# Turning six of eight token tiles to channel-major by VectorE block transposes and transfers inside SBUF

## The chip, the cores and the metric

The kernel runs on one core of a Trainium2 chip. The metric is the device time of one execution in microseconds; the time before is the median of three runs. Work is done by TensorE (PE: matrix products and transposes, with its weight load PEld), VectorE (DVE), ScalarE (ACT), GpSimd (POOL), and by transfers that are issued mostly from SyncE's queue (SP). Everything runs in float32, where a product of two matrices is made of three products of their high and low parts.

## The reference, cut to what matters

One decoder layer on 16 meta tokens and 1024 sequence tokens with 1024 channels. The change lies between the output projection with its LayerNorm and the up-projection of the feed-forward net:

```python
mixed = sigmoid(g_attn) * y_attn + sigmoid(g_conv) * y_conv
h = layer_norm(ALPHA * h + mixed @ w_out, ln1_g, ln1_b)
up = causal_dwconv(h @ ffn_w_up, ffn_dw, ffn_dw_b)        # 3 taps over tokens
u, g = split(up, 2)
f = (gelu(g) * u) @ ffn_w_down
return layer_norm(ALPHA * h + f, ln2_g, ln2_b)
```

The LayerNorm runs over channels, so it wants tokens on the partitions and channels along the row. The product `h @ ffn_w_up` contracts over channels, so it wants channels on the partitions. Between the two, `h` must be turned.

## The kernel before, in words

The stage `w_out` takes the 1024 sequence tokens as eight tiles of 128, in the written order 3, 7, 2, (-1), 6, 0, 4, 1, 5; "-1" is the pair of rows that the convolution needs from before the sequence. For each tile `out_rows` loads its residual row tile from DRAM into one of two places in `RT` (the first half of `OB`), makes the product in two halves of 512 channels on TensorE (`product`, line 1339, 24 products of 512 columns a half), adds the residual and takes statistics on VectorE (lines 1342 and 1343), normalises the tile (line 1364), and stores it to DRAM (`h1d`) for the later residual.

`turn` then turns a normalised tile: eight 128x128 transposes on TensorE (line 1378) into two banks of PSUM, and eight ScalarE activations (line 1388) that apply the gain and bias of the LayerNorm, which are now one number per partition, and write into `FA` (`h1F(sub, h, k)`). A tile's turn is emitted inside the next tile's `out_rows`, behind the product of one of its halves: `behind=[last]` puts the transposes after that product in TensorE's order, and the next half's first product after them. The list `ahead` says which tile is due. Tile 5, the last, is turned in the first pass of the up-projection.

`FA` holds `h` for two halves of the tokens, `sub` 1 (tiles 2, 3, 6, 7) and `sub` 0 (the two edge rows, tiles 0, 4, 1, 5); tiles 0 to 3 have h = 0 and tiles 4 to 7 have h = 1. The up-projection is a two-by-two block scheme with seven products in place of eight: B11, B21, B22 are blocks of `h` (a half of the channels for one h), and BT1 to BT4 are sums of blocks. `form_t2`, `form_t3` and `form_t4` make the sums on VectorE (line 1288), and `split_of` splits each operand into a high part (ScalarE, line 1279) and a low part (VectorE, line 1284). `form_t2` subtracts first B11 from B12 and then B11 from B22, so it needs all channels of the tiles with h = 1. EARLY is the first half of `sub` 0, tiles 0 and 4; LATE is tiles 1 and 5.

Three things set the order of work around the change:

- `rank(...)` gives instructions a priority (smaller goes first) by which the builder orders each engine's queue against its own estimate of the times. The queue it writes is then executed in order.
- `line(ins)` chains instructions: each is put after the one lined before it in VectorE's order. The sums and statistics of tiles 0, 4, 1 and 5 are lined (`pin`, line 1334), and so are the low parts, the sums of blocks, and the first splits of the up-projection's weights. The dictionary `work` says which of them is emitted between the two halves of which tile:

```python
    work = {0: [(w_first, 2), (split_of, 1, B11), (split_of, 1, B21), (split_of, 1, B22)],
            4: [(w_first, 3), (split_of, 1, BT2), (w_first, 3), (form_t4, 1)],
            1: [(form_t3, 1), (split_of, 0, B11, EARLY), (form_t2, 0, EARLY), (w_first, 5)],
            5: [(w_first, 6)]}
```

- Places in SBUF: the second half of `OB` holds `T2_AT` and, for tile -1, its two rows (columns 3072 to 4095); `OC` and `RHC` hold later the operands of `sub` 1 (`B_AT`).

The products of a half wait for one of three PSUM banks with the tag "mm". Every load and store of this stage is issued from SP (line 113).

Of the kernel before, what the change touches and what calls it, by code (L numbers as in the profile page):

```python
# [25 lines left out]
AF = mybir.ActivationFunctionType  # L26
# [3 lines left out]
P = 128  # L30
D = 1024
KC = D // P
# [29 lines left out]
SUB = [(0, 258), (258, HW)]  # L62


RK_TURN, RK_SPLIT, RK_EVAC, RK_START, RK_QKV, RK_RESID, RK_ATT = 450, 500, 600, 1000, 10000, 20000, 30000
# [36 lines left out]
def tile_hybrid_layer(  # L102
# [3 lines left out]
    nc = tc.nc  # L106
# [5 lines left out]
    def load(o, i):  # L112
        return nc.sync.dma_start(out=o, in_=i)
# [5 lines left out]
    def f32(ap):  # L119
        return ap.bitcast(F)  # L120

    def after(ins, first):

        tc.add_manual_dep(ins.ins, first.ins.name, mybir.DependencyInfo(
            mybir.DependencyClass.NoSync, mybir.DependencyReason.SCHED_ONLY), reason="order of work")

    @contextmanager
    def rank(p):

        saved = tc.cur_priority  # L130
        tc.cur_priority = p
        yield
        tc.cur_priority = saved
# [10 lines left out]
    RHC = arena.tile([P, 8384], R, name="RHC")  # L144
    RHO = arena.tile([P, 8384], R, name="RHO")
    OB = arena.tile([P, 4 * U], F, name="OB")
# [49 lines left out]
    cols = const.tile([P, N_COLS], F, name="cols")  # L196
# [19 lines left out]
    g1col = lambda k: colA[:, 58 + k:59 + k]  # L216
    b1col = lambda k: colA[:, 66 + k:67 + k]
# [60 lines left out]
    def split(raw, hi, lo, quick=False, behind=None):  # L278
        ins = nc.scalar.copy(hi, raw)  # L279
        if behind is not None:  # L280
            after(ins, behind)
        return (nc.vector if quick else nc.gpsimd).tensor_tensor(lo, raw, f32(hi), OP.subtract)  # L282
# [391 lines left out]
    bias = ap.tile([P, 2, NH // 2, KW], F, name="bias")  # L674
# [58 lines left out]
    for r in range(2):  # L733
        rows = slice(r * HD, (r + 1) * HD)
# [13 lines left out]
    src = ps[:16, :P].rearrange("p (g d) -> p g d", d=HD)  # L748
    nc.scalar.copy(VA[:16, 0, :, 0], src)
    nc.vector.tensor_tensor(VA[:16, 0, :, 1], src, f32(VA[:16, 0, :, 0]), OP.subtract)  # L750
    for q4 in range(2):
# [4 lines left out]
        src = ps[:, :].rearrange("p (n g d) -> p n g d", g=2, d=HD)  # L756
# [16 lines left out]
    def load_q(g, i):  # L773
        m = 0 if i else 16
        t = ap.tile([P, 8 * P + 16], R, name="qt", tag="qt", bufs=3)[:, 16 - m:]
        for h in range(2):
            load(f32(t[h * HD:(h + 1) * HD]), dram(qd, g * HD * 8 * U + q_at(i) - m, [[8 * U, HD], [1, 8 * P + m]]))
        if m:
            pairs0.append(t[:, :16].rearrange("p (l r q) -> p l r q", l=2, r=4))
        return t[:, m:].rearrange("p (u l h x) -> p l u h x", l=2, u=2, h=2)  # L780
# [7 lines left out]
    ahead = chunks_done[first_chunk + 2 * KC + 7]  # L788
# [6 lines left out]
    for h in range(NH):  # L795
        g, r = divmod(h, 4)
        o = ps[:2, h * 16:(h + 1) * 16]
# [34 lines left out]
    for g in range(NKV):  # L832
# [3 lines left out]
        src = ps[:16].rearrange("p (r q) -> p r q", r=4)[:, :, 0:2]  # L836
# [3 lines left out]
    for g in range(NKV):  # L840
        o = po[:, g * 8:g * 8 + 8]
# [21 lines left out]
    for i in range(NB):  # L863
        for g in range(NKV):
            q = load_q(g, i) if i else q0[g]
# [6 lines left out]
            for u in range(2):  # L872
# [3 lines left out]
                for h in range(2):  # L876
                    o = ps[:, h * KW:h * KW + w]
# [8 lines left out]
                if not i:  # L886
                    f = first[u]
                    src = ps[:, :2 * KW].rearrange("p (h c) -> p h c", h=2)
# [9 lines left out]
            for h in range(2):  # L898
                for u in range(2):
                    j = h * 2 + u  # L900
# [68 lines left out]
    OC = late.tile([P, 8320], R, name="OC")  # L969
# [169 lines left out]
    def two_rows(k, behind=None):  # L1139

        for t, a in enumerate(two_sum):
            m = pair[:, k, t:t + 1]
            if k == 0:
                nc.scalar.activation(a, wo_raw[k], AF.Copy, scale=m)
                continue
            ins = nc.vector.scalar_tensor_tensor(a, wo_raw[k], m, a, OP.mult, OP.add)
            if behind is not None:
                after(ins, behind)
# [74 lines left out]
    def h1_at(sub, i):  # L1223
        return 2048 * sub + i * (SUB[sub][1] - SUB[sub][0])

    def h1F(sub, h, k):
        o = h1_at(sub, h * KC + k)
        return FA[:, o:h1_at(sub, h * KC + k + 1)]
# [28 lines left out]
    def line(ins):  # L1257

        if lined:
            after(ins, lined[-1])  # L1260
        lined.append(ins)
        return ins
# [9 lines left out]
    def bsplit(sub, q, src, cs=slice(None)):  # L1272
        with rank(RK_SUMS):
            a = columns(sub, q)[0] - SUB[sub][0]
            x, y, _ = cs.indices(SUB[sub][1] - SUB[sub][0])
            x = max(x, a)
            hi, lo = (wide(bsum(sub, q, hl))[:, :, x - a:y - a] for hl in range(2))
            src = wide(src)[:, :, x:y]
            ins = nc.scalar.copy(hi, src)
            if (sub, q) in ((0, BT2), (0, BT4), (0, BT1), (0, BT3)):  # L1280
                if high:
                    after(ins, high[-1])
                high.append(ins)
            line(nc.vector.tensor_tensor(lo, src, f32(hi), OP.subtract))
# [5 lines left out]
    def blocks(sub):  # L1290

        return [quadrant(sub, kk, h) for kk in range(2) for h in range(2)]
# [3 lines left out]
    def form_t2(sub, cs=slice(None)):  # L1296
        b11, b12, b21, b22 = blocks(sub)
        bsub(b11, b12, b11, cs)
        bsub(T2_AT[:, :b22.shape[1]], b22, b11, cs)

    def form_t3(sub, cs=slice(None)):
        b11, b12, b21, b22 = blocks(sub)
        bsub(b12, b22, b12, cs)

    def form_t4(sub, cs=slice(None)):
        b11, b12, b21, b22 = blocks(sub)
        bsub(b21, T2_AT[:, :b22.shape[1]], b21, cs)

    def split_of(sub, q, cs=slice(None)):
        b11, b12, b21, b22 = blocks(sub)  # L1310
        src = {B11: b11, B21: b21, BT2: T2_AT[:, :b22.shape[1]], BT4: b21, BT1: b11, BT3: b12, B22: b22}[q]
        bsplit(sub, q, src, cs)
# [76 lines left out]
        return behind[-1] if behind else None  # L1389


    RING = [RHO[:, i * 1024:(i + 1) * 1024] for i in range(4)]
    RING += [None] * 4
    RING += [RHO[:, 6208 + i * 1024:6208 + (i + 1) * 1024] for i in range(2)]
    ring_next, W2 = [0], []

    def wsplit(src):
# [4 lines left out]
        else:  # L1402
            i = (i - 2) % len(RING)
            if RING[i] is None:
                RING[i] = wsp_p.tile([P, D], R, name="ws", tag=("whi", "wlo")[i % 2])
            t = RING[i]
        hi, lo = t[:, 0:512], t[:, 512:1024]
# [59 lines left out]
    def edges():  # L1467
        with rank(RK_TURN):
            first, second = (FA[:, h * 2064:h * 2064 + 2064].rearrange("p (k n) -> p k n", n=258)[:, :, 0:2]
                             for h in range(2))  # L1470
            for t, c, op in ((edge, 58, OP.mult), (first, 66, OP.add)):
                line(nc.vector.tensor_tensor(first, t, colA[:, c:c + KC].unsqueeze(2).to_broadcast([P, KC, 2]), op))
            nc.vector.memset(second, 0.0)

    ahead = []
# [4 lines left out]
    for i in (3, 7, 2, -1, 6, 0, 4, 1, 5):  # L1480
        if i == -1:
            out_rows(i)
            continue
        rows = out_rows(i, ahead, work.get(i, ()))
        ahead = [None, (i, *rows)] if i == 3 else [(i, *rows)]
        if i == 3:
            two_rows(7, rows[2])
        if i == 7:
            for a, (hi, lo) in zip(two_sum, two_parts):
                after(split(a, hi, lo, True), rows[2])  # L1490
            two_stack.close()
            W2.append(wo_stack.enter_context(tc.tile_pool(name="w2", bufs=1, side="right", reuse_waits="tile")).tile(
                [P, 2048], R, name="W2"))
        if i == 0:
            form_t2(1)
        if i == 4:
            split_of(1, BT4)
            split_of(1, BT1)
            edges()
        if i == 1:  # L1500
            split_of(1, BT3)
            split_of(0, B21, EARLY)
            form_t3(0, EARLY)
            form_t4(0, EARLY)
# [64 lines left out]
    for c in range(FC):  # L1569
# [8 lines left out]
        for subs in passes:  # L1578
            last = subs == passes[-1]
            w_next = iter(range(7))  # L1580
            a, b = SUB[subs[0]][0], SUB[subs[-1]][1]
            i = max(a, 2)

            def at(t, a=a):
                return t[:, 254 + a:254 + b]
# [19 lines left out]
            def tt(*x):  # L1605
                with rank(RK_CHAIN):
                    return nc.vector.tensor_tensor(*x)
# [12 lines left out]
            ins = tt(c11[:, a:b], at(Z), u13[:, a:b], OP.add)  # L1620
# [23 lines left out]
            ins = tt(c22[:, i:b], c22[:, i:b], u13[:, i:b], OP.add)  # L1644
# [127 lines left out]
    rows, stats = {}, {}  # L1772
# [158 lines left out]
```

## Time and profile before

| | |
|---|---|
| median of 3 runs | 1236.12 us (1236.04 to 1236.16) |
| span of the profiled execution, first to last instruction | 1234.6 us |
| the profiled execution's own time beside it | not listed apart; the span is 1.5 us below the median |
| busy PE / DVE / ACT | 99% / 88% / 47% of the span |
| stage `w_out` (products from about 500 us, first up-projection product) | to 589.4 us |
| products of the up-projection | 589.4 to about 1017 us |
| products of the down-projection | 1017 us to the end |

A line of the trace's timeline gives the start and length in us, the engine, the line of the kernel, the operation, output <- inputs, shapes, how many such instructions follow each other (x8), and in brackets the idle time before it and what released it. A group line gives durations in ns as minimum/median/maximum. Records of TensorE overlap, since its products are pipelined: how far apart they start says more than how long each one lasts.

### The profile page before, as it was taken

The page shows a single profiled execution, that of the slowest core. Times are in us where ns is not written, and L with a number is a line of the kernel's source. Part 1 is how long each engine was busy: PE and PEld are TensorE (multiplying, and loading weights), DVE is VectorE, ACT ScalarE, POOL GpSimd, SP SyncE. Part 2 cuts the span into 40 slices and gives each one's busy share as a digit, 9 for nine tenths or more (in the row PEclk, how much of TensorE's full clock was granted, in tenths as well). Part 3 has the DMA queues.
Part 4 walks back from the last instruction along what each step waited for, and adds up shares of the span by engine and source line. Part 5 has one row for each costly group of instructions (what it writes and reads, how often), then busy time and mean ns, then how long its engine had stood idle before and what let it go on. Part 6 is the DMA issues. An engine that isn't in the chain of part 4 may idle for free.

```text
span 1234.6 us, 21810 instructions
## 1 busy us (share of the span) xinstructions
PE 1225.2 (99%) x8568; PEld 1141.5 (92%) x8568; DVE 1085.2 (88%) x1842; ACT 584.7 (47%) x1065; POOL 15.6 (1%) x20
## 2 busy tenths in 40 slices
PE   9999999999999999999999999999999999999997
PEld 8999989999999999888999999999999998888886
DVE  8899989999879798659899999998999986996697
ACT  7532336654255223345755545555455554445331
POOL 1000000000000010000000000000000000000000
PEclk9999999999999999999999999999999999999999
DMA  7396834412255655322255555554455568988722
GB/s 282 74 298 151 210 98 116 127 55 73 82 158 163 183 140 144 104 85 87 66 171 207 191 187 205 188 183 142 172 203 190 178 239 304 391 315 312 256 86 85
DMA packets 109152, 213.02 MB, mean 173 GB/s; under 512 B 31883, under 2 KB 46779, under 8 KB 108922
## 3 DMA queue, kind: packets, MB, share of 16 engines
q1 hardware_dynamic: 93050, 200.56, 49.5%
q10 hardware_dynamic: 16000, 11.07, 2.9%
q8 instruction: 67, 1.10, 0.4%
q14 instruction: 35, 0.29, 0.1%
HBM read 149.98 MB, written 62.70 MB: 172 GB/s over the span
## 4 chain that ended last, share of the span: by engine, by line
PE 98%; DVE 1%; ACT 0%; issue 0%; DMA 0%; POOL 0%; DVEq 0%; POOLq 0%
PE px L1599 14%; PE py L1599 9%; PE ps_x L1745 9%; PE ps_z L315 8%; PE ps_z L314 8%; PE ps_z L310 8%; PE ps_z L1745 8%; PE pw L1599 5%; PE pz L1599 5%; PE ps_p L310 2%; PE ps_p L314 2%; PE ps_p L315 2%; PE ps_w L310 2%; PE ps_w L315 2%; PE ps_w L314 2%; PE ps_z L550 2%
## 5 line engine op out<-in xcount | busy, mean ns | idle before, releaser
L707 DVE SCALAR_TENSOR_TENSOR FA<-cin,cols,FA 128x1026 f32<-128x1026 f32 x120 | 152.2, 1277 | 0.9
L315 PE MATMUL ps_z<-RHO,wlo 128*128 128x256 f32 (+2 forms) x324 | 103.5, 320 | 0.0
L314 PE MATMUL ps_z<-RHO,whi 128*128 128x256 f32 (+2 forms) x324 | 103.4, 319 | 0.0
L315 PE MATMUL ps_z<-RHC,wlo 128*128 128x256 f32 (+2 forms) x324 | 103.4, 319 | 0.0
L314 PE MATMUL ps_z<-RHC,whi 128*128 128x256 f32 (+2 forms) x324 | 103.4, 319 | 0.0
L310 PE MATMUL ps_z<-RHO,whi 128*128 128x256 f32 (+2 forms) x324 | 103.3, 319 | 0.0
L310 PE MATMUL ps_z<-RHC,whi 128*128 128x256 f32 (+2 forms) x324 | 103.2, 319 | 0.0
L279 ACT CAST whi<-wr 128x1024 fp32r<-128x1024 f32 x37 | 38.9, 1050 | 107.4 <-PE ps_z L314 85.5
L1408 ACT CAST RHO<-wr 128x512 fp32r<-128x512 f32 x92 | 55.3, 619 | 25.3 <-DVE wr L1426 11.7
L1409 DVE TENSOR_TENSOR RHO<-wr,RHO 128x512 fp32r<-128x512 f32 x92 | 61.8, 684 | 5.1 <-ACT RHO L1408 5.0
L310 PEld LDWEIGHTS ps_z<-RHO,whi 128*128 128x128 f32 x324 | 60.9, 188 | 4.3
L314 PEld LDWEIGHTS ps_z<-RHO,whi 128*128 128x128 f32 x324 | 61.0, 188 | 4.2
L310 PEld LDWEIGHTS ps_z<-RHC,whi 128*128 128x128 f32 x324 | 60.9, 188 | 4.1
L314 PEld LDWEIGHTS ps_z<-RHC,whi 128*128 128x128 f32 x324 | 61.0, 188 | 4.0
L315 PEld LDWEIGHTS ps_z<-RHO,wlo 128*128 128x128 f32 x324 | 60.9, 188 | 4.0
L315 PEld LDWEIGHTS ps_z<-RHC,wlo 128*128 128x128 f32 x324 | 61.0, 188 | 3.9
L1426 DVE TENSOR_TENSOR wr<-wr 128x512 f32<-128x512 f32 x88 | 59.9, 681 | 0.2
L282 DVE TENSOR_TENSOR wlo<-wr,whi 128x1024 fp32r<-128x1024 f32 x35 | 42.7, 1220 | 11.8 <-ACT whi L279 11.4
L1611 ACT COPY FA<-px 128x514 f32<-128x514 f32 (+2 forms) x23 | 13.2, 572 | 70.7 <-PE px L1599 70.6
L1408 ACT CAST ws<-wr 128x512 fp32r<-128x512 f32 x60 | 36.1, 618 | 18.8 <-DVE wr L1426 10.7
L714 ACT ACTIVATE FA<-ps_z,cols 128x258 f32<-128x258 f32 (+2 forms) x48 | 26.1, 544 | 39.4 <-PE ps_z L315 36.6
L1599 PE MATMUL px<-OA,RHO 128*128 128x258 f32 (+1 forms) x336 | 43.8, 279 | 0.0
(491 smaller groups left out, 3488.2 us busy)
## 6 DMA issues: line engine op xcount, KB each, us to landing
wr<-in_w_up_dram SPq DMA_DIRECT2D x44, 512.0 KB, 4.6
wr<-in_w_z_dram SPq DMA_DIRECT2D x30, 512.0 KB, 3.9
fd<-FA SPq DMA_DIRECT2D x44, 256.0 KB, 2.4
OB<-in_w_down_dram SPq DMA_DIRECT2D x19, 512.0 KB
qt<-qd SPq DMA_DIRECT2D x28, 256.0 KB, 4.1
td<-OB SPq DMA_DIRECT2D x12, 512.0 KB
sums<-fd SPq DMA_DIRECT2D x12, 512.0 KB, 7.6
sd<-sums SPq DMA_DIRECT2D x12, 512.0 KB
```

Of the source, the lines that this page charges most:

```text
L279: ins = nc.scalar.copy(hi, raw)
L282: return (nc.vector if quick else nc.gpsimd).tensor_tensor(lo, raw, f32(hi), OP.subtract)
L310: ins = nc.tensor.matmul(ps, ah, bh, start=i == 0, stop=False)
L314: nc.tensor.matmul(ps, ah, bl, start=False, stop=False)
L315: last = nc.tensor.matmul(ps, al, bh, start=False, stop=i == n - 1)
L707: nc.vector.scalar_tensor_tensor(acc[c], cin[:, j:j + U], wc, acc[c], OP.mult, OP.add)
L714: nc.scalar.activation(t, ps, AF.Tanh, bias=bcol(14 + i), scale=0.5)
L1408: nc.scalar.copy(hi, src)
L1409: ins = nc.vector.tensor_tensor(lo, src, f32(hi), OP.subtract)
L1426: ins = nc.vector.tensor_tensor(*x)
L1599: ins = nc.tensor.matmul(o, x[:, ks], bmat(sub, q, hl, k), start=first and k + j == 0, stop=k == 3 and j == 2, skip_group_check=not first)
L1745: nc.tensor.matmul(bank[:, cs], l[:, ts], r[:, ws], start=first and a and x + k == 0, stop=z and x == len(ops) - 1 and k == 2, skip_group_ ...
```

## The change

Six tiles (3, 7, 2, 6, 0 and 4) are no longer turned by TensorE. The new `turn_dma` does it in three steps:

1. One VectorE transpose of the tile's 1024 columns in blocks of 32x32, written into a block of 1024 columns in the second half of `OB` (columns 2048 on for tiles 3, 7, 2 and 6, columns 3072 on for tiles 0 and 4). Each 32x32 block is turned in place; the blocks of one row of partitions hold 32 tokens.
2. Sixteen transfers within SBUF, issued from SP, each of 32 partitions with 1 KB: they bring the 4x4 arrangement of blocks into its turned order, in a place of the tile's own in `OC` or `RHC` that is free then.
3. The same eight ScalarE activations as before, now with SBUF as the source and with four runs of 32 columns each.

The tiles 1 and 5 are turned as before. The list `ahead` stays empty where the last tile was turned in the new way. For tiles 0 and 4 the VectorE transpose is lined; tile 0's stands right behind its normalisation, tile 4's behind the low parts of BT4 and BT1 of `sub` 1.

```diff
+    TURN_AT = {3: (OC, 4144, 2048), 7: (OC, 5168, 2048), 2: (OC, 6192, 2048), 6: (OC, 7216, 2048), 0: (RHC, 2096, 3072), 4: (RHC, 3120, 3072)}
+
+    def turn_dma(i, r):
+        t, o, b = TURN_AT[i]
+        blocks, cols = OB[:, b:b + 1024], f32(t[:, o:o + 1024])
+        with rank(RK_TURN):
+            ins = nc.vector.transpose(blocks.rearrange("p (q k j) -> p q k j", q=4, k=KC),
+                                      r.rearrange("p (k q j) -> p q k j", k=KC, q=4))
+            if i in (0, 4):
+                line(ins)
+            for a in range(4):
+                for q in range(4):
+                    load(cols[32 * q:32 * q + 32, a * 256:(a + 1) * 256],
+                         blocks[32 * a:32 * a + 32, q * 256:(q + 1) * 256])
+            h, jj = divmod(i, 4)
+            sub = 0 if jj < 2 else 1
+            a = 2 + jj * P - SUB[sub][0]
+            src = cols.rearrange("p (a k j) -> p k a j", a=4, k=KC)
+            for k in range(KC):
+                nc.scalar.activation(h1F(sub, h, k)[:, a:a + P].rearrange("p (a j) -> p a j", a=4), src[:, k],
+                                     AF.Identity, bias=b1col(k), scale=g1col(k))
...
         rows = out_rows(i, ahead, work.get(i, ()))
-        ahead = [None, (i, *rows)] if i == 3 else [(i, *rows)]
+        ahead = [] if i in TURN_AT else [(i, *rows)]
+        if i in TURN_AT and i != 4:
+            turn_dma(i, rows[0])
         if i == 3:
             two_rows(7, rows[2])
...
         if i == 4:
             split_of(1, BT4)
             split_of(1, BT1)
+            turn_dma(i, rows[0])
             edges()
```

## The prediction

> **What bounds the kernel now.** I read the page's head and its chain of waits first, then a table of busy time by stage around the change, then the timelines of TensorE, VectorE, ScalarE and the DMA queue there.
>
> ```profile
> span 1234.6 us, 21810 instructions
> PE 1225.2 (99%) x8568; PEld 1141.5 (92%) x8568; DVE 1085.2 (88%) x1842; ACT 584.7 (47%) x1065; POOL 15.6 (1%) x20
> PE 98%; DVE 1%; ACT 0%; issue 0%; DMA 0%; POOL 0%; DVEq 0%; POOLq 0%
> ...
> 542.00:554.00 12.00, 12.00 (x58) 10.03 (x57) 8.87 (x14) 4.77 (x11) 0.00 (x0) 1.00 0.39 103
> 554.00:566.00 12.00, 12.00 (x58) 10.02 (x57) 10.81 (x17) 6.74 (x14) 0.00 (x0) 1.00 0.25 89
> 566.00:578.00 12.00, 12.00 (x58) 10.03 (x57) 11.24 (x21) 6.35 (x13) 0.00 (x0) 1.00 0.23 88
> 578.00:592.00 14.00, 14.00 (x78) 12.10 (x78) 10.59 (x20) 6.36 (x17) 0.00 (x0) 1.00 0.23 77
> ```
>
> TensorE sets the time, 98% of the chain. But the four stage rows (columns: stretch, length, busy PE, PEld, DVE, ACT, POOL, clock, DMA share, GB/s) say something that the average of 88% hides: from 554 to 578 us VectorE is busy 22.05 of 24 us. The stage of the change has two nearly full engines; time taken off one can be used only as far as the other keeps up. The clock is 1.00 throughout and plays no part.
>
> **What TensorE gives back.** Columns: start, length, engine, line, operands.
>
> ```profile
> 521.98 0.40 PE L315 MATMUL ps_w<-whi,RHC 128*128 128x512 f32 x1
> 522.22 1.04 PE L1378 MATMUL ps_h<-cols,OB 128*128 128x128 f32 x8
> 523.01 0.48 PE L310 MATMUL ps_w<-RX,RHC 128*128 128x512 f32 x1
> 523.33 0.40 PE L314 MATMUL ps_w<-RX,RHC 128*128 128x512 f32 x1
> ...
> 583.03 1.03 PE L1378 MATMUL ps_h<-cols,OB 128*128 128x128 f32 x8
> ```
>
> Products start every 0.227 us elsewhere in this listing. Around one tile's eight transposes, the third product after 521.98 starts at 523.33, 1.35 us later, where two steps are 0.45: a turn costs TensorE 0.9 us, not the 8 x 0.27 that its records last. Three turns (3, 7, 2) stand ahead of tile 6's normalisation; those of 6, 0 and 4 stand behind the first halves of tiles 0, 4 and 1. Removing the six gives 6 x 0.9 = 5.4 us, 2.7 us of it before tile 0's first half is ready, all of it before tile 1's turn at 583.03. So 5.4 us (0.44%) is the ceiling.
>
> **What VectorE leaves of it.** From tile 0 on, VectorE's work is pinned one behind the other (`line`): every entry below waits for the one above.
>
> ```profile
> 545.03 0.81 DVE L1364 TENSOR_SCALAR OB<-OB,mv,sd 128x1024 f32<-128x1024 f32 x1
> 547.88 0.69 DVE L1342 TENSOR_TENSOR OB<-ps_w,OB 128x512 f32<-128x512 f32 x1 [2.03 <-PE ps_w L315]
> ...
> 549.21 1.27 DVE L1409 TENSOR_TENSOR W<-wr,W 128x512 fp32r<-128x512 f32 x2
> 550.41 2.35 DVE L1284 TENSOR_TENSOR OC<-FA,OC 128x1024 fp32r<-128x1024 f32 x2
> 552.68 1.22 DVE L1284 TENSOR_TENSOR RHC<-FA,RHC 128x1024 fp32r<-128x1024 f32 x1
> 554.22 0.69 DVE L1342 TENSOR_TENSOR OB<-ps_w,OB 128x512 f32<-128x512 f32 x1 [0.32 <-PE ps_w L315]
> ...
> 564.12 1.22 DVE L1284 TENSOR_TENSOR OC<-OB,OC 128x1024 fp32r<-128x1024 f32 x1
> ...
> 571.74 1.22 DVE L1284 TENSOR_TENSOR OC<-FA,OC 128x1024 fp32r<-128x1024 f32 x1
> 572.88 0.17 DVE L1472 TENSOR_TENSOR FA<-edge,cols 128x16 f32<-128x16 f32 x1
> ...
> 574.50 1.21 DVE L1288 TENSOR_TENSOR FA<-FA 128x1024 f32<-128x1024 f32 x1
> 575.82 0.70 DVE L1284 TENSOR_TENSOR RHC<-FA,RHC 128x520 fp32r<-128x520 f32 x1
> 576.56 0.70 DVE L1288 TENSOR_TENSOR FA<-FA 128x520 f32<-128x520 f32 x1
> 577.29 0.70 DVE L1288 TENSOR_TENSOR OB<-FA 128x520 f32<-128x520 f32 x1
> ...
> 581.11 0.81 DVE L1364 TENSOR_SCALAR OB<-OB,mv,sd 128x1024 f32<-128x1024 f32 x1
> ```
>
> The last row is tile 1's normalisation, ending at 581.92; TensorE transposes tile 1 at 583.03, so today VectorE is 1.1 us early. From 547.88 to 581.92 is 34.04 us of pinned work, with one wait for TensorE in it (0.32). The change lets it begin 2.7 us earlier (545.2), drops the 0.32, and adds the block transposes of tiles 0 and 4.
>
> A block transpose of 128x1024 fp32 isn't in the trace. Nearest rows: 1.22 us (L1284, same elements, two tensors) and 0.81 us (L1364, one tensor). Bounds: 0.81, and 2.44 if it took two passes. I take 1.22, one element a step like most of VectorE's rows.
>
> With no other wait, tile 1 is normalised at 545.2 + 34.04 - 0.32 + 2.44 = 581.4, and TensorE turns it there instead of at 583.03: gain 1.6 us, not 5.4. TensorE waits for VectorE first.
>
> **What the new way takes.** Of each turn's steps, after the block transpose: 16 transfers (32 partitions x 1 KB) issued one by one from SP, the last one's landing, then eight ScalarE evacuations, each reading all 16 pieces.
>
> ```profile
> L113 SPq DMA_DIRECT2D ed<-OB x1: 244/244/244, 536.2 to 536.2; - x1
> L113 SPq DMA_DIRECT2D v1d<-vrow x1: 297/297/297, 62.6 to 62.6; - x1
> L113 SPq DMA_DIRECT2D OB<-h0d x8: 319/320/341, 499.2 to 573.4; - x8
> L113 SPq DMA_DIRECT2D FA<-kd x4: 453/548/587, 53.3 to 61.3; - x4
> ...
> qd<-qsh SPq DMA_DIRECT2D x4, 1.0 KB, 1.8
> out_dram<-r SPq DMA_DIRECT2D x16, 256.0 KB, 2.0
> OB<-h0d SPq DMA_DIRECT2D x8, 512.0 KB, 3.2
> ...
> 496.59 0.42 ACT L1191 ACTIVATE RHC<-OB 128x256 fp32r<-128x256 f32 x1 [1.62 <-DVE OB L1186]
> 548.31 2.90 ACT L1388 ACTIVATE FA<-ps_h,cols 128x128 f32<-128x128 f32 x8 [3.90 <-PE ps_h L1378]
> 551.25 1.05 ACT L1279 CAST RHC<-FA 128x1024 fp32r<-128x1024 f32 x1
> ```
>
> The issue time (ns, min/median/max) hardly follows the size: 244 for 2 rows, 297 for 8, 320 for 128, 453 at least for 64. I take 0.33 a transfer with the gap, as 32 rows lie between the 8 and the 128; ends 0.244 and 0.453. Landing (last column, us): 1.8 for 1 KB to 3.2 for 512 KB; I take 2.0. So the lag from the end of a block transpose to the last landing is D = 16 x 0.33 + 2.0 = 7.3 us (5.7 to 10.4). The evacuations stay at 2.90 us for eight (SBUF source, by the 0.42 row at most 3.4). On the old path the first followed the transposes at once.
>
> Two pinned VectorE entries need a turn that comes late:
>
> - **Wait A, tile 6.** 552.68 (L1284 into RHC) is the low part of B22 of the second half, which needs all of tiles 6 and 7 and ScalarE's cast (1.05). VectorE gets there 4.80 us after its start: 545.2 + 4.8 = 550.0. Tile 6's normalisation ends at 545.84 - 2.7 = 543.1, its transpose at 544.35, so B22 is ready at 544.35 + D + 2.90 + 1.05 + 0.1 = 548.4 + D. Wait: D - 1.6 = 5.7 us.
> - **Wait B, tile 4.** Its transpose is pinned behind the entry at 571.74; 3.7 us of old work (572.88 to 576.56) and 0.7 (first subtraction) cover it before the second `form_t2` subtraction (577.29), which needs all of tile 4: wait D + 2.9 - 4.4 = D - 1.5 = 5.8 us.
>
> Behind both stand tile 1's second-half sum, its normalisation and so the transposes at 583.03, for which TensorE waits in order, as tile 5's second half is tied behind them. Sum: 5.7 + 5.8 - 1.6 = +9.9 us (2D - 4.7). Ends by D: +6.7 to +16.1; a transpose of 0.81 or 2.44 shifts by -1.2 or +3.7 (three of them lie in these sums), slower evacuations by +1.0.
>
> Other pieces, with their cover. The tiles' shared OB block makes tile 7's transpose wait for tile 3's landing (512.8, the end of its normalisation, + 1.2 + 7.3 = 521.3); behind it on VectorE stand the two edge-row splits, needed by TensorE's products with `sel`:
>
> ```profile
> 511.98 0.80 DVE L1364 TENSOR_SCALAR OB<-OB,mv,sd 128x1024 f32<-128x1024 f32 x1
> ...
> 519.92 2.36 DVE L282 TENSOR_TENSOR OC<-two,OC 128x1024 fp32r<-128x1024 f32 x2
> ...
> 528.56 2.02 PE L1353 MATMUL ps_w<-OC,sel 128*2 128x512 f32 x8
> ...
> 534.10 0.81 DVE L1364 TENSOR_SCALAR OB<-OB,mv,sd 128x1024 f32<-128x1024 f32 x1
> ```
>
> They end at 521.3 + 1.2 + 2.4 = 524.9, the products now come at 526.8: nothing, 1.9 us spare. SP issues 96 more transfers (32 us in some 66), ahead of the loads of residual rows: tile 2's normalisation (534.9 - 1.8) plus 1.2 and 16 x 0.33 ends the issue at 539.6, tile 0's rows then land at about 543.1 (0.3 + 3.2), needed at 545.2; without those 2 us a late load adds its excess. The added 3.1 MB lie in stages with a DMA share of 0.23 to 0.39. POOL has no work here. After tile 5 all moves with TensorE; I find nothing that gives the loss back.
>
> Median: 1236.12 against a span of 1234.6; I add the 9.9 to the median: **1246.0 us**.
>
> **A rule against the row.** The trace's issues take 0.244 to 0.32 us each, 16 of them 3.9 to 5.1, more than a landing of 2.0. The Trainium skill, "DMA: Bandwidth & Descriptors", section "Issuing engines are not separate DMA queues", has it that the time a sequencer spends on starting a DMA is usually small relative to the DMA itself. By that rule the change would come out at no change, the first rival below; by the trace's rows 16 small transfers in a row are bound by it.
>
> **Rivals.**
> 1. *Issue costs nothing in a row* (no change). If issues ran on unseen and D were one landing of 2.0, waits A and B would be 0.4 + 0.5, the sum -0.7: 1235.4. It decides at D = 2.35. For it: an issue isn't work of a compute engine. Against: no row below 0.244. The same end comes if TensorE's order in the built program puts the first up-projection products into the wait and the lag is at its low end (part of this 0.15).
> 2. *TensorE bound* (faster). If the pinned list stayed ahead, all 5.4 us would come: 1230.7. It needs both waits away and 3.8 us off the list. For it: 98% of the chain is TensorE's. Against: the list has no idle time to give.
> 3. *ScalarE's queue* (slower still). If tile 0's evacuations are put ahead of the cast for the entry at 564.12 (BT2), that cast ends at 561.5 + 7.3 + 2.9 + 1.05 = 572.8 where VectorE arrives at 568.0: another 4.7 us, 1250.7. It needs a builder that thinks a turn short by 5 us.
>
> **How the numbers follow.** Forecast 0.59, rival 1 0.15, rival 2 0.09, rival 3 (with the dear transposes) 0.17. The measurement can tell 0.2%, 2.5 us. Slower: 0.59 + 0.17 = 0.76; within 0.15; faster 0.09. The forecast's own range is 1241 to 1252 (D from 5.7 to 9, transposes either way). The range given, 1235 to 1254, takes in rival 1 and most of rival 3.
>
> **What would show it.** Right: TensorE idle once, before L1378 of tile 1, some 10 us longer than it should be, its releaser VectorE; VectorE idle 4 to 8 us before the L1284 into RHC and before the second L1288 of 520 columns, released by ScalarE; ScalarE waiting for transfers; SP issues at 0.24 to 0.45 us, 16 in a row. Wrong: issues pipelined well under 0.2 us; the two entries released before VectorE comes; TensorE's idle time unchanged.

## The result, and the profile after

The changed kernel takes 1270.69 us (median; 1269.9 to 1272.13) against 1236.09 (median of four runs) for the kernel before: ratio 1.028, interval 1.0268 to 1.0292, +34.6 us. The forecast was +9.9: right in sign and in kind, too small by a factor of 3.5, and the time lies outside its range.

The head of the page after, and the first line of its chain of waits:

```profile
span 1270.2 us, 21893 instructions
PE 1228.9 (97%) x8520; PEld 1141.7 (90%) x8520; DVE 1091.3 (86%) x1848; ACT 587.0 (46%) x1065; POOL 15.6 (1%) x20
...
PE 90%; SPq 4%; DVE 2%; DMA 2%; ACT 1%; issue 1%; DVEq 0%; ACTq 0%
```

TensorE's busy time hardly moved (1225.2 before), its share of the chain fell from 98% to 90%, and SP's *queue*, which did not appear before, holds 4%, the largest part of what TensorE lost. These are the issues. SP's timeline after (start, length, engine, line, operands, count), with the group line of those issues (ns, minimum/median/maximum) and the landing time of the last column (us):

```profile
516.28 10.29 SPq L113 DMA_DIRECT2D OC<-OB  x16
529.44 10.02 SPq L113 DMA_DIRECT2D OC<-OB  x16
544.13 10.01 SPq L113 DMA_DIRECT2D OC<-OB  x16
556.98 10.02 SPq L113 DMA_DIRECT2D OC<-OB  x16
567.04 0.58 SPq L113 DMA_DIRECT2D OB<-h0d  x1
578.67 10.64 SPq L113 DMA_DIRECT2D RHC<-OB  x16
596.13 10.01 SPq L113 DMA_DIRECT2D RHC<-OB  x16
...
L113 SPq DMA_DIRECT2D OC<-OB x64: 507/589/597, 516.3 to 566.4; - x64
...
OC<-OB SPq DMA_DIRECT2D x64, 32.0 KB, 1.8
```

Sixteen issues take 10.0 to 10.6 us: 0.59 us each and 0.04 between, 0.63 where 0.33 was taken. The row of 0.58 at 567.04 is a load of residual rows right behind sixteen of them; the same load took 0.32 before. The landing (1.8) was sized rightly. So the lag D of one turn is 16 x 0.63 + 1.8 = 11.9 us, not 7.3. The first four turns follow each other every 13 to 15 us with little between. VectorE after shows what that does (in brackets the idle time before and its releaser), with the two ScalarE rows that end the lags of tiles 0 and 4:

```profile
514.94 1.24 DVE L1398 STREAM_TRANSPOSE OB<-OB 128x1024 f32<-128x1024 f32 x1
528.17 1.25 DVE L1398 STREAM_TRANSPOSE OB<-OB 128x1024 f32<-128x1024 f32 x1 [6.41 <-DMA OC<-OB]
542.86 1.25 DVE L1398 STREAM_TRANSPOSE OB<-OB 128x1024 f32<-128x1024 f32 x1 [3.76 <-DMA OC<-OB]
555.71 1.25 DVE L1398 STREAM_TRANSPOSE OB<-OB 128x1024 f32<-128x1024 f32 x1 [5.75 <-DMA OC<-OB]
561.30 0.69 DVE L1342 TENSOR_TENSOR OB<-ps_w,OB 128x512 f32<-128x512 f32 x1 [4.35 <-DMA OB<-h0d]
572.76 1.23 DVE L1284 TENSOR_TENSOR RHC<-FA,RHC 128x1024 fp32r<-128x1024 f32 x1 [6.57 <-ACT RHC L1279]
591.28 0.16 DVE L261 SCALAR_TENSOR_TENSOR sd<-mv,sd 128x1 f32<-128x1 f32 x1 [1.70 <-ACT sd L253]
609.26 0.70 DVE L1288 TENSOR_TENSOR FA<-FA 128x520 f32<-128x520 f32 x1 [9.83 <-ACT FA L1411]
610.79 0.70 DVE L1288 TENSOR_TENSOR OB<-FA 128x520 f32<-128x520 f32 x1 [0.84 <-ACT FA L1411]
...
590.57 0.49 ACT L1411 ACTIVATE FA<-RHC,cols 128x128 f32<-128x128 f32 x1 [1.48 <-DMA RHC<-OB]
607.58 3.18 ACT L1411 ACTIVATE FA<-RHC,cols 128x128 f32<-128x128 f32 x8 [7.68 <-DMA RHC<-OB]
```

The rows of L1398 are the block transposes of tiles 3, 7, 2 and 6. Those of tiles 7, 2 and 6 each wait for the transfers of the tile before, which still read the shared block in `OB`. Tile 6's block transpose ends at 556.96, and the low part of B22 (L1284 into RHC) starts at 572.76, where it was at 552.68 before: +20.1. Then comes wait B, 9.83 + 0.84 = 10.7 (L1288), and 1.7 at tile 4's normalisation, whose ScalarE step L253 stands behind tile 0's evacuations. With the two pinned transposes of tiles 0 and 4 (2.4 together), less the old 0.32 wait and VectorE's old lead of 1.1, these make 20.1 + 10.7 + 1.7 + 2.4 - 0.3 - 1.1 = 33.5. TensorE's rows show where it arrives:

```profile
574.64 0.79 PE L310 MATMUL ps_w<-RX,RHO 128*128 128x512 f32 x1 [6.82 <-DVE OB L1342]
615.48 1.97 PE L1378 MATMUL ps_h<-cols,OB 128*128 128x128 f32 x8 [21.08 <-DVE OB L1364]
624.54 1.58 PE L1624 MATMUL px<-OC,W 128*128 128x256 f32 x12
```

Tile 1's turn is at 615.48 instead of 583.03, +32.45, 1 us less than the sum. Of that 1 us, 0.36 is the part of the 1.7 that stood at tile 4's normalisation before too (569.29 there); the rest is gaps of 0.1 to 0.3 us in VectorE's old list, one of them before 565.53, that have closed. So the new wait at L253 is 1.3 us. From tile 1's turn to the first up-projection product 9.06 us pass, 6.33 before (583.03 to 589.36). The stage table after says why (busy PE, PEld, DVE, ACT, POOL, then the granted clock, DMA share, GB/s):

```profile
592.00:604.00 12.00, 2.40 (x11) 1.66 (x9) 7.39 (x11) 4.15 (x9) 0.00 (x0) 0.72 0.25 80
604.00:616.00 12.00, 0.52 (x3) 0.52 (x4) 5.37 (x11) 3.48 (x9) 0.00 (x0) 0.50 0.19 57
616.00:628.00 12.00, 12.00 (x61) 10.53 (x60) 7.60 (x16) 6.24 (x15) 0.00 (x0) 0.78 0.25 88
```

During the long idle time the granted clock drops to 0.50, and TensorE resumes at that clock: another 2.7 us. 32.45 + 2.7 = 35.2, against a span that is 35.6 longer.

### The profile page after: what moved, and what is told of

It reads as the page before. It is cut to its first block, busy times and chain, and to the rows that moved or that the text cites. A ratio compares the mean times of both kernels' runs of the same rounds, so it can differ in the third digit from the quotient of the medians.

```text
span 1270.2 us, 21893 instructions
## 1 busy us (share of the span) xinstructions
PE 1228.9 (97%) x8520; PEld 1141.7 (90%) x8520; DVE 1091.3 (86%) x1848; ACT 587.0 (46%) x1065; POOL 15.6 (1%) x20
## 4 chain that ended last, share of the span: by engine, by line
PE 90%; SPq 4%; DVE 2%; DMA 2%; ACT 1%; issue 1%; DVEq 0%; ACTq 0%
PE px L1624 14%; PE ps_x L1770 9%; PE py L1624 9%; PE ps_z L315 8%; PE ps_z L314 8%; PE ps_z L310 8%; PE ps_z L1770 7%; PE pw L1624 5%; PE pz L1624 5%; SPq L113 4%; PE ps_p L310 2%; PE ps_p L314 2%; PE ps_p L315 2%; PE ps_z L550 2%; PE ps_o L928 1%; PE ps_s L879 1%
## 5 line engine op out<-in xcount | busy, mean ns | idle before, releaser
L282 DVE TENSOR_TENSOR wlo<-wr,whi 128x1024 fp32r<-128x1024 f32 x35 | 42.7, 1221 | 11.8 <-ACT whi L279 11.4
L1430 ACT CAST ws<-wr 128x512 fp32r<-128x512 f32 x60 | 36.2, 619 | 17.8 <-DVE wr L1448 10.7
```

## The experiments

A time that stands without a ratio was measured once. Repeated runs of one kernel here lie up to 3 us apart (tile 3 alone: 1238.65 to 1241.7), so a difference of 1 or 2 us between single runs shows nothing by itself.

The theory after the result: an issue from SBUF to SBUF costs 0.63 us of its queue whatever it moves, so a turn has a lag of 12 us, and the loss is that lag at the places where a turn is wanted or stands in another's way. The rivals were the data (1 KB pieces, bytes), the shared `OB` block, the late residual rows, ScalarE's order, and the clock.

**Prices.** No layer is computed here, only groups of transfers, with nothing beside them.

```diff
+    group("s32x1K", 32, 256, 16, shift=32)     # 16 x (32 partitions x 1 KB), SBUF to SBUF
+    group("s8x1K", 8, ...)  ...  group("s128x1K", 128, 256, 16)
+    group("s32x4K", ...)  group("s32x128B", ...)
+    group("r128x1K", 128, 256, 16, "ds")       # from DRAM;  "sd": to DRAM
+    group("act32x1K", ..., eng=nc.scalar)  group("pool32x1K", ..., eng=nc.gpsimd)
```

> A kernel of transfers alone, no layer is computed: groups of transfers of one shape, each group issued back to back and waited for before the next. In the changed kernel an issue took 0.59 us with 0.04 us to the next. Theory 'price of the issue': the 16 transfers of 32 partitions x 1 KB inside SBUF cost about 0.59 us of SP's queue each here too, with nothing else running; 128 partitions x 4 KB between SBUF and DRAM cost 0.32. Rival 'busy transfer engines': alone, the same 16 transfers issue at 0.25 to 0.35 us each, and the 0.59 comes from the loads and stores beside them. The groups by size (8, 16, 32, 64, 128 partitions; 128 B, 1 KB, 4 KB a row), by side (SBUF to SBUF, to DRAM, from DRAM) and by queue (SP, ACT, POOL) are to tell what the price hangs on.

Group lines of this run (ns; the name tells rows and bytes per row; `dt` is DRAM):

```profile
L133 SPq DMA_DIRECT2D dt<-src x20: 338/419/1186, 141.5 to 167.8; - x20
L133 SPq DMA_DIRECT2D s32x1K<-src x16: 583/590/598, 19.0 to 28.5; - x16
...
L133 SPq DMA_DIRECT2D s128x1K<-src x16: 478/599/601, 90.3 to 99.9; - x16
L133 SPq DMA_DIRECT2D s32x128B<-src x16: 507/588/590, 128.0 to 137.4; - x16
...
L133 SPq DMA_DIRECT2D r128x1K<-dt x16: 319/430/523, 187.4 to 194.7; - x16
L133 ACTq DMA_DIRECT2D act32x1K<-src x16: 541/602/602, 200.3 to 209.8; - x16
L133 POOL DMA_DIRECT2D pool32x1K<-src x16: 501/505/636, 214.4 to 244.5; - x16
```

0.59 to 0.60 us for 4 KB (32 x 128 B) as for 128 KB, with no other engine at work, and the same from ScalarE's queue. With DRAM on one side the median is 0.42 to 0.43 in this run. From POOL the starts are 2.0 us apart (16 of 32 KB, from 214.4 to 244.5). So up to 128 KB the price belongs to the issue and not to its bytes (four of 512 KB took 0.8 us each), and a smaller number of transfers lowers what a turn pays; the run with two queues below shows a second way. The profile before already had issues in a row on SP's queue:

```profile
89.46 5.86 SPq L113 DMA_DIRECT2D bias<-vd  x9
...
95.92 1.64 SPq L113 DMA_DIRECT2D va<-va  x2
97.66 1.49 SPq L113 DMA_DIRECT2D va<-v  x2
```

The nine loads from DRAM (`vd`) take 0.65 us each, so DRAM on one side does not always make an issue cheaper; the four transfers inside SBUF (`va`) take 0.7 to 0.9 each.

**One transfer a turn.** One transfer of 128 x 4 KB takes the place of the sixteen; the 4x4 rearrangement is left out.

```diff
-            for a in range(4):
-                for q in range(4):
-                    load(cols[...], blocks[...])
+            load(cols, blocks)
```

> The changed kernel with one transfer of 128 partitions x 4 KB in place of each turn's 16: the rearrangement of the blocks is left out, the same bytes move, and the six block transposes on VectorE and all evacuations stay. Theory 'number of issues': the lag from block transpose to landing falls from 11.9 us to about 0.4 + 2.4 = 2.8, the waits of VectorE fall to 1.2 and 1.3 us, residual rows come in time, and the time is 1236.1 + 2 x 2.8 - 4.7 = 1237 us (1235 to 1240). Rival 'VectorE's added work and the SBUF-sourced evacuations' (6 x 1.25 + 48 x 0.04 us): unchanged in this kernel, so most of the 34.6 us would stay, over 1255. Rival 'bytes moved inside SBUF': also over 1255.

1243.71 us, 4 to 7 us over what was expected. 27.0 of the 34.6 us hang on the number of issues. These are two rows of SP's queue in this run:

```profile
516.73 0.59 SPq L113 DMA_DIRECT2D OB<-h0d  x1
...
546.94 0.47 SPq L113 DMA_DIRECT2D OC<-OB  x1
```

An SBUF-to-SBUF issue that stands alone takes 0.47 to 0.50 us (512 KB), and not 0.59; the least of the changed kernel's issues of 32 KB is 0.51. And the load of residual rows, 0.32 us where it stands alone, takes 0.59 right behind such an issue. So two things go into the price here: the memory on the two sides, and whether the issue stands in a row. What stays in this run is a lag of 3.1 to 4.3 us and the same waits, smaller (VectorE, then TensorE):

```profile
545.08 0.68 DVE L1342 TENSOR_TENSOR OB<-ps_w,OB 128x512 f32<-128x512 f32 x1
554.43 1.22 DVE L1284 TENSOR_TENSOR RHC<-FA,RHC 128x1024 fp32r<-128x1024 f32 x1 [3.48 <-ACT RHC L1279]
582.25 0.70 DVE L1288 TENSOR_TENSOR FA<-FA 128x520 f32<-128x520 f32 x1 [1.94 <-ACT FA L1408]
588.47 1.97 PE L1378 MATMUL ps_h<-cols,OB 128*128 128x128 f32 x8 [10.93 <-DVE OB L1364]
```

Tile 0's first sum comes at 545.08, as the prediction assumed (545.2) for turns that stand in nobody's way. Yet tile 6's normalisation waits 2.6 us for ScalarE behind evacuations, and TensorE still pauses long enough to start slow (1.97 instead of 1.03 for eight transposes).

**Each place alone.** Tile 4 alone, tile 6 alone, and tiles 3, 7 and 2 are turned the new way; the others by TensorE.

```diff
-    TURN_AT = {3: ..., 7: ..., 2: ..., 6: ..., 0: ..., 4: ...}
+    TURN_AT = {4: ...}          # or {6: ...}, or {3: ..., 7: ..., 2: ...}
```

> Only tile 4 is turned by block transpose and transfers; the other five are back on TensorE. Theory 'lag on the pinned list': no queue of turns before it, so only wait B: VectorE idles 11.9 - 1.5 = 10.4 us before the second form_t2 subtraction of 520 columns, tile 1's normalisation ends at 581.9 + 1.25 + 10.4 = 593.6 instead of 581.9, TensorE idles some 11 us before tile 1's transposes, and with the lower granted clock after such a pause (about 2.5 us) the time is 1248 to 1251. Rival 'only many turns together jam the queue': one turn alone is covered, within 3 us of 1236.

> Only tile 6 turned the new way, with its 16 transfers; the rest on TensorE. Theory: wait A alone. Its block transpose ends near 547.1 us, lands 11.9 us later, B22's high part is ready at 563, and VectorE, which is there at 552.7, waits 10.4 us; TensorE waits in turn and the time is 1245 to 1249. Rival 'wait A only binds behind the jam of the earlier turns': under 1240.

> Only tiles 3, 7 and 2 are turned the new way; 6, 0 and 4 are back on TensorE, so neither wait A nor wait B (tile 6, tile 4) has a late turn in it. Theory 'SP's queue': three times 16 issues of 0.63 us stand ahead of the residual rows' loads, tile 0's rows land near 559 us instead of 543, its sum starts about 11 us late and the time is 1243 to 1250. Rival 'only the two pinned waits cost': with them gone the three turns' 2.7 us of TensorE come through, 1233 to 1236.

1248.62, 1247.77 and 1248.13 us: +12.4, +11.7 and +11.9 over the runs of the kernel before beside them, all three as expected. Tile 4 alone shows wait B (9.89 + 0.84 us at L1288), tile 6 alone wait A (10.26 us at L1284 into RHC). With 3, 7 and 2 VectorE's waits for residual rows (OB<-h0d) add to 14 us, the longest 10.71 before tile 0's first sum. Each place costs about one lag.

**Loads of residual rows out of SP's queue**, with tiles 3, 7 and 2, and with all six.

```diff
-            load(whole, h0d[u:u + n, :])
+            store(whole, h0d[u:u + n, :])      # issues from ScalarE's queue
```

> Tiles 3, 7 and 2 turned the new way (as in only_372, 1248.1 us), and the residual rows' loads are issued from ScalarE's queue instead of SP's, so that no 16 issues stand ahead of them. Theory 'SP's queue delays the residual rows': VectorE's 14.1 us of waits for these loads go, tile 0's first sum is back near 547 us, and the time is 1235.5 to 1239 (2.7 us of TensorE saved, some 3 us lost at the edge rows, where one ScalarE copy stands behind a tile's evacuations). Rival 'the shared OB block alone' (tile 7's transpose waits for tile 3's landing, tile 2's for tile 7's): the loads don't matter and it stays within 2 us of 1248.

> All six tiles turned the new way (as in the changed kernel, 1270.7 us), with the residual rows' loads on ScalarE's queue. Theory 'four turns in a row': tiles 3, 7, 2 and 6 go one after the other through SP and one OB block, 1.25 + 10.1 + 1.8 us each from 515 us on, so tile 6's evacuations still start near 568 us whatever the loads do, wait A grows by what the start gains, and the time stays within 4 us of 1270.7. Rival 'late residual rows cost the 16 us by which tile 0's first sum is late': the time falls by 10 us or more, to 1260 or less.

With three tiles 1247.58 us: my theory that the rows behind SP's issues are the cost fell, and the rival on record, that moving the loads changes nothing (within 2 us of 1248), has the number. Tile 0's sum came back to 548.00, and the next need took over: `split_of(1, B11)` wants tile 2, whose transfers were the third in the series:

```profile
548.00 0.69 DVE L1342 TENSOR_TENSOR OB<-ps_w,OB 128x512 f32<-128x512 f32 x1 [3.79 <-DMA OB<-h0d]
560.86 2.36 DVE L1284 TENSOR_TENSOR OC<-FA,OC 128x1024 fp32r<-128x1024 f32 x2 [10.25 <-ACT OC L1279]
```

With six 1269.1 us, as expected. Here tile 0's sum is at 548.10 instead of 561.30, yet the low part of B22 starts at 572.89 (572.76 in the changed kernel), with 10.50 us of wait instead of 6.57. So the 20.1 us there are set by the series of four turns through one block and one queue. Late rows and wait A are two views of them, and taking one away hands the time to the other. Of the 13 to 15 us from one turn to the next the queue alone holds 10; no run gives each tile a block of its own, so how the rest is shared between block and queue is not shown.

**Two queues.** Half of the sixteen issues go from ScalarE's queue.

```diff
-                    load(cols[...], blocks[...])
+                    (load, store)[q % 2](cols[...], blocks[...])
```

> The changed kernel with half of each turn's 16 transfers issued from ScalarE's queue, the other half from SP's. Theory 'the price is the issuing queue's': each queue takes 8 x 0.63 = 5.1 us, the lag is 6.9 us and the time 1247 to 1258 (2 x 6.9 - 4.7 = 9.1 us, plus some 2 us of lower clock, plus what 5 us of issues a turn delay ScalarE's own work). Rival 'the transfer hardware takes 0.63 us for each, whoever issues': the issues on both queues stretch to about 1.2 us, the lag stays at 12 us and the time at 1268 or more.

1255.11 us, as expected: 15.6 us come back with the same transfers, bytes and block. Eight issues take 5.0 to 7.7 us on SP. The Trainium skill, "Perfetto Trace Analysis", section "DMA Optimizations", says that spreading transfers over the engines that can start them may help where making their descriptors is the limit; this run agrees. It is no cure: 19 us of the loss stay, and ScalarE, which evacuates the turns, now issues too.

**The clock.** With tile 4 alone, 48 products of no use fill TensorE's pause.

```diff
+                if i == 5 and half == 0:
+                    for j in range(WARM):      # WARM = 48
+                        ins = nc.tensor.matmul(idle, wo[0][0][:, 0:P], wo[0][0][:, 0:512], ...)
```

> As only_4 (1248.6 us; TensorE waits 11.4 us before tile 1's transposes), with 48 idle products of 512 columns (10.9 us, their sum is used by nothing) put into that wait. Theory 'a TensorE that waits is granted half the clock for its next 5 us': tile 1's eight transposes take 1.03 us instead of 1.94, the products after them come every 0.227 us instead of 0.427, and the time falls by 2 to 3 us, to 1246 (1245.5 to 1247), although work was added. Rival 'the slow steps come from something else after the wait (late operands)': no change or slower, 1248.5 or more.

1247.66 us against 1248.62, half of the least gain that was expected. With one run of each, that 1 us is not clear of noise. The trace is what shows the clock: the granted clock stayed 1.00 throughout, and from tile 1's turn to the first up product the time is 6.37 us instead of 8.17. Of these 1.8 us, 0.7 come back as waits for ScalarE inside the first up products (0.41 and 0.30). The clock is real, a secondary cost of 1 to 2 us in this pause. Stage rows of tile 4 alone (the clock is the third number from the end), whose TensorE is idle from 582.1 to 593.5:

```profile
584.00:586.00 2.00, 0.00 (x0) 0.00 (x0) 0.00 (x0) 0.52 (x2) 0.00 (x0) 1.00 0.44 92
586.00:588.00 2.00, 0.00 (x0) 0.00 (x0) 0.70 (x1) 2.00 (x6) 0.00 (x0) 0.74 0.52 207
...
594.00:596.00 2.00, 2.00 (x9) 1.88 (x8) 2.00 (x4) 1.40 (x5) 0.00 (x0) 0.50 0.65 262
596.00:598.00 2.00, 2.00 (x8) 1.55 (x6) 1.97 (x4) 2.00 (x7) 0.00 (x0) 0.70 0.01 4
598.00:600.00 2.00, 2.00 (x10) 1.67 (x9) 0.82 (x2) 0.69 (x3) 0.00 (x0) 1.00 0.29 82
```

The clock falls some 4 to 5 us into the pause and is back about 4 us after work resumes. The Trainium skill, "TensorE: Matmul & The Clock Gate", section "Part 1: The HAM clock gate", has the clock halved after at least one idle window of about 3.4 us and back after one busy window of that length; these rows agree with both.

**Through DRAM.** To have fewer issues: one store of the blocks to DRAM and four loads of 128 rows x 1 KB that gather them; for all six tiles, for 3, 7 and 2, and for 3 and 2.

```diff
+            load(tb[i], blocks)
             for a in range(4):
-                for q in range(4):
-                    load(cols[32 * q:32 * q + 32, a * 256:(a + 1) * 256], blocks[...])
+                load(cols[:, a * 256:(a + 1) * 256], dram(tb[i], 32 * a * D, [[256, 4], [D, 32], [1, 256]]))
```

> All six tiles turned the new way, but the blocks go out to DRAM in one store of 128 x 4 KB and come back in four loads of 128 x 1 KB, 5 issues in place of 16: 0.32 + 2.4 (landing, which SP waits for) + 4 x 0.43 + 2.4 = 6.9 us from block transpose to landing. Theory 'the lag and nothing else': with the lag that the prediction had assumed (7.3 us) its sum comes true: 1236.1 + 2 x 6.9 - 4.7 = 1245, plus 2 us of lower TensorE clock and 1 to 3 us of ScalarE's order, 1246 to 1251. Rival 'transfers in SBUF are what is slow, DRAM is not' would need the lag to be shorter than 5 us: 1243 or less. Rival 'the loss isn't the lag's': 1258 or more.

> Only tiles 3, 7 and 2, by way of DRAM (5 issues, 6.9 us a turn). These tiles' values are needed from 547 us on, so the three turns (ends near 526, 530 and 545 us with their evacuations) are covered, and SP is held 4.5 us a turn. Theory 'a turn that nobody waits for gives its 0.9 us': 1233.5 to 1235, a ratio of 0.998 to 0.999. Rival 'ScalarE's evacuations of tile 7 get between the copies of the edge rows and TensorE idles 2 to 3 us there': 1235.5 to 1237.

> Only tiles 3 and 2, by way of DRAM; tile 7, whose evacuations come at the edge rows' time, stays on TensorE. Theory: two covered turns give 1.8 us, 1234.0 to 1234.8 (ratio 0.9985 to 0.999). Rival 'the pinned list of VectorE bounds the end from tile 0 on, so that an earlier start is lost there': no change, 1235.8 to 1236.5.

All three missed: 1279.89; 1249.04 (ratio 1.0106, 1.009 to 1.0121); 1244.16 (1.0062, 1.0049 to 1.0075). I had reckoned a lag of 6.9 us. With tiles 3 and 2 the trace has 12.5 to 12.9: tile 2's block transpose ends at 538.1, SP issues the four loads from 540.85 to 543.06, and they have landed only when ScalarE starts at 550.65. Five issues in place of sixteen save 7 us, and the store, its wait and a landing of 6.0 (tile 3) and 7.6 us (tile 2) give that back. The time of the six tiles came where the rival on record had put it, that the loss isn't the lag's (1258 or more); but the lag of 6.9 us was not there, so that rival is not tested by it.

**Covered turns.** Tile 3 alone, tiles 3 and 7, these two with the residual rows on ScalarE's queue, and the kernel before with nothing but its residual rows on that queue.

```diff
-    TURN_AT = {3: ..., 7: ..., 2: ..., 6: ..., 0: ..., 4: ...}
+    TURN_AT = {3: ..., 7: ...}      # or {3: ...}; rows_37 and rows_0: store(whole, h0d[...])
```

> Tile 3 alone is turned by transfers; it ends its lag of 12 us at about 529 and its channels are wanted only at about 550, and no other turn follows it through the shared block. Theory (a turn costs its lag only where it is wanted; elsewhere TensorE keeps its 0.9 us): 1235.2 us, 0.9 below the kernel before, 1234.6 to 1235.8; no added wait over 0.5 us on VectorE before 560. Rival 1 (the transpose on VectorE takes back what TensorE gains): 1236 to 1237. Rival 2 (the 16 issues on SP delay the residual rows of tile 2 or 6 even so): 1237 or more, with a wait for OB<-h0d on VectorE.

> Tiles 3 and 7: two turns in a row, the second's lag ends at about 541. Theory: 1234.3 us (1.8 below the kernel before), 1233.8 to 1236; the rows of tile 0 are loaded by SP behind the second turn's issues (end about 541) and land at about 544.5, against a start of 545.2 to 547.9 of tile 0's first sum. Rival (the rows are late, as with three turns): tile 0's first sum starts after 549, 1237 to 1240.

> As with tiles 3 and 7 alone, with the loads of residual rows issued from ScalarE's queue. Theory: 1234.3 us, 1233.8 to 1236, the same as with SP. Rival (the loads stand behind the evacuations of tile 7 in ScalarE's order and come late): tile 0's first sum starts after 549, 1237 to 1240.

> The kernel before with the loads of residual rows issued from ScalarE's queue, no tile turned by transfers: what moving the loads does by itself. Theory: no change, 1235.6 to 1236.6. Rival: ScalarE's order makes rows late, 1237 or more.

Tile 3 alone 1241.12 us (ratio 1.0038, 1.0025 to 1.0051) and 3 with 7 1240.35 (1.0035, 1.0022 to 1.0048): both slower, where 1235.2 and 1234.3 were expected. With the rows moved, 1235.18 (0.9994, 0.9985 to 1.0002). The kernel before with its rows moved, 1236.04 (1.0, 0.9991 to 1.0009). So even one turn that is wanted by nobody for 20 us costs 5 us while SP has the residual rows behind its issues. Tile 3 alone, on SP, VectorE and TensorE:

```profile
516.18 10.29 SPq L113 DMA_DIRECT2D OC<-OB  x16
527.14 2.88 SPq L113 DMA_DIRECT2D OB<-h0d  x2
...
531.34 1.29 DVE L1342 TENSOR_TENSOR OB<-ps_w,OB 128x512 f32<-128x512 f32 x2 [9.69 <-DMA OB<-h0d]
...
531.73 1.87 PE L1353 MATMUL ps_w<-OC,sel 128*2 128x512 f32 x4 [3.21 <-ACT OB L1355]
...
533.00:536.00 3.00, 3.00 (x9) 2.33 (x8) 2.74 (x6) 0.77 (x2) 0.00 (x0) 0.50 0.00 0
```

The two loads of residual rows that were issued at 518.3 and 523.5 before now follow at 527.1, behind the sixteen issues, and VectorE waits 9.69 us for tile 2's. ScalarE's copies of the edge rows (L1355) stand behind tile 3's evacuations, TensorE waits 3.21 us for them, and comes back at half the clock: its next products start every 0.43 us until 537.2 (ten of them, 2 us lost). With the rows moved, the copies come before the evacuations, both waits are gone (which of the two the move cures first is not separated), and the gain of a covered turn can be seen at last:

```profile
547.07 0.69 DVE L1342 TENSOR_TENSOR OB<-ps_w,OB 128x512 f32<-128x512 f32 x1 [2.46 <-DMA OB<-h0d]
...
569.75 1.06 PE L1378 MATMUL ps_h<-cols,OB 128*128 128x128 f32 x8 [0.39 <-DVE OB L1364]
...
581.57 1.03 PE L1378 MATMUL ps_h<-cols,OB 128*128 128x128 f32 x8
```

Tile 1's turn is at 581.57, 1.46 us earlier than before (583.03), of which 0.2 come with the move of the rows alone (582.84 there). Two turns give back 1.3 us there, not the 1.8 expected. The 1.8 did arise: at tile 2's turn (533.87 against 535.71 with the rows alone moved) and through tile 0's (557.43 against 559.28) TensorE is 1.84 and 1.85 us ahead, 0.92 a turn. It loses 0.55 of it at tile 4's turn (569.75 against 571.05), where it waits for VectorE's normalisation. VectorE's pinned list began only 0.6 us earlier (547.07 against 547.69), behind tile 0's rows, which are late again by 2.46; that these rows keep VectorE back is read from that one row and was not tried. The median is 0.95 us lower, and its interval takes in no change. This is the best version that I found; it is not shown to be faster than the kernel before.

## Why the prediction was right or wrong

- **Wrong: the price of an issue** (0.33 us, "as 32 rows lie between the 8 and the 128"). The rows that I interpolated all have DRAM on one side. Measured: 0.63 to 0.67 with the gap, for 8 to 128 rows and for 128 B to 4 KB a row. My upper bound of 0.453 did not hold it either; it is the least of the FA<-kd row, whose median is 0.548. D was 12 and not 7.3. In the formula 2D - 4.7 this gives +19.3, so it explains 9 of the 25 us that were missed. Nearer rows stood in the profile before (bias<-vd, va<-va and va<-v, shown with the prices above): at 0.65 us an issue they give D = 16 x 0.65 + 2.0 = 12.4 and +20, so this term could have been had before the run.
- **Wrong: "SP issues 96 more transfers ... nothing" and "nothing, 1.9 us spare"** for the turns that share the `OB` block. Both were worked out with D = 7.3 and one turn at a time. With 10 us of issue and 1.8 of landing each, four turns in a row, 13 to 15 us apart, are longer than the products they hide behind (a tile's products take 11.8 us in the profile before, 547.67 to 559.46): tile 7's transpose started at 528.17 where 521.3 was forecast, and so on, to B22 at 572.76 where 550.0 + 5.7 = 555.7 was forecast: 17.1 us, the largest part (4.7 of it are what the longer D adds to wait A, counted in the point above). The run with all rows moved shows that the series sets it, not how block and queue share it; the one-tile run shows that SP's order alone costs 5.
- **Put at nothing: TensorE's clock after a pause**, 2.7 us in the changed kernel. The prediction says that the clock "plays no part", read from a stage without pauses.
- **Rival 3's mechanism, elsewhere and small**: ScalarE's order costs 1.3 us (L253 behind tile 0's evacuations), and not at BT2.
- **Right**: the block transpose (1.22 taken, 1.245 measured) and the landing (2.0; 1.8). That TensorE waits for VectorE's pinned list is right too: with tile 4 alone a wait of 10.7 us on that list puts tile 1's turn 10.45 us later (593.48 against 583.03). That the list would leave 1.6 us of the gain if it had no waits was not tested. Waits A and B are where and about as large as their formulas say: with D = 12, wait B should be 10.5 and is 10.7, and A is 10.3 in the run of tile 6 alone (10.4). TensorE's gain is sized rightly: two covered turns put it 0.92 us a turn ahead, of which 0.65 a turn are left where it has to wait for VectorE, the second full engine that the prediction names. So the 5.4 us stand as a ceiling.
- **Wrong: the range.** Its ends fall short of the sum's own: +16.1, +3.7 and +1.0 reach 1257, past the 1254 that was given (and D = 9 with the dear transposes gives 1253, not 1252); the time measured lies 14 us beyond that, and D = 12 in the same formula gives only 1255.4.
- **The rule on issue time** (the Trainium skill, "DMA: Bandwidth & Descriptors", section "Issuing engines are not separate DMA queues"): sixteen issues of 10.1 us before a landing of 1.8 contradict "usually small" for transfers of 32 KB, and the measurement decides. Rival 1, to which that rule led, is refuted by the 0.63 us an issue in the changed kernel, and by the two-queue run.

## What to carry to other kernels

Price a small transfer by the queue that issues it, from a row with the same kind of memory on both sides and with as many issues one behind the other, and count what stands behind it on that queue: sixteen issues of 0.63 us are 10 us in which no load gets out. A lag that "lies beside other work" must be checked for all its repetitions in a row, through each block and queue that they share, not once. When taking one wait away moves the time by nothing, look for the next need of the same late data before giving up the cause.

## What the runs showed of the hardware

In a row, an issue from SBUF to SBUF takes 0.59 to 0.60 us from SP's queue (4 to 128 KB) or ScalarE's (32 KB), and about 2.0 us from POOL (32 KB); one that stands alone takes 0.47 to 0.50 from SP. A load from DRAM that takes 0.32 us alone takes 0.59 right behind such an issue. A pause of TensorE of only 3.2 us was followed by ten products at half the clock. Four gathered loads of 128 x 1 KB from DRAM landed 6.0 and 7.6 us after the last issue, where 512 KB of whole rows land in 3.2 (OB<-h0d in the profile before).
